# Weights and columns of a float32r matmul stream at other addresses, and its three passes in another order

## The chip, the cores and the metric

The kernel runs on one core of a Trainium2 chip. The metric is the device time of one execution in microseconds (us). Several executions are timed; one of them, a separate one, is profiled.

## What is computed

The reference is the trunk of a two-layer encoder. It has 272 positions (16 meta tokens ahead of 256 inputs), each of 2,048 features, in float32. Layer 0 mixes with a state-space scan, layer 1 with an attention that takes its keys and values from the output of layer 0; each is followed by a gated feed-forward stage. At the end the 16 meta positions are dropped.

```python
h = concatenate([meta, x])                                   # 272 x 2048
h = h + ssd_mixer(rmsnorm(h))                                # in_proj 2048 -> 10304, scan, out_proj 4096 -> 2048
h = h + (silu(u @ w_gate) * (u @ w_up)) @ w_down             # 2048 -> 2 x 5632 -> 2048
k, v = rmsnorm(h) @ w_kv                                     # 2048 -> 2 x 2048
h = h + stick_breaking_attention(rmsnorm(h) @ w_q, k, v) @ w_o
h = h + swiglu(rmsnorm(h))                                   # the second feed-forward stage
return rmsnorm(h)[16:]
```

Nearly all of the arithmetic is in the products with weight matrices.

## The kernel before, in words

The kernel keeps features on the 128 partitions and positions along the free dimension. A weight matrix is cut into 128x128 tiles. One output tile (128 features by all positions) is the sum over the K tiles of the contraction: K is 16 for an input of 2,048 features, 44 for the hidden layer of a feed-forward stage, 8 for a piece of the out projection.

**Three passes.** A float32 product is made of three float32r products. Every weight tile w is split into wh (rounded) and wl (the rest), every input x into xh and xl, and `mac` (L108 to L112) adds wh·xh (L110), wh·xl (L111) and wl·xh (L112) into one accumulator. Each `PE.matmul` is two instructions of TensorE: a load of 128x128 weights (LDWEIGHTS, engine PEld in the profile) and a matmul (PE) that streams the columns of x through them. While a matmul streams, the load of the next one's weights runs. So the load beside the pass on L110 is that of wh once more, the load beside L111 is that of wl, and the load beside L112 is that of the next tile's wh.

**Where the weights come from.** `load` (L91) brings eight weight tiles, 512 KB, into one of five `raw` buffers through the SP queue. `halves` (L99) makes `hi` with a copy on ScalarE (L101) into one of five buffers, and `lo` with a subtraction on VectorE (L103) into one of four. `project` (L114) makes one output tile, `project_block` (L130) several together. All engines run through their own instructions in order; a scheduler in the build decides that order, and waits on semaphores tie the engines together.

**The inputs.** They are held split, as one tile of shape [128, K, 2, n]: for each k first the n columns of xh, then the n columns of xl. `split_scaled` (L150) writes them for u, the input of each stage. Other inputs are y (output of the scan), hid (hidden layer), ukv (input of keys and values), uq (of the queries) and ob (output of the attention). n is 272 (T) in layer 0 and for keys and values, and 256 (SEQ) for queries, attention and the second feed-forward stage.

**Addresses in a partition.** A weight tile has 512 bytes, and `hi` and `lo` buffers start at 81,920 and 102,400 plus multiples of 4,096. So every load of weights starts at a multiple of 256 bytes. u and ukv start at 26,624 (0 beyond a multiple of 256), hid and uq at 126,400 (192 beyond), ob at 159,168 (192), the two y tiles at 132,672 and 150,080 (64). With 256 columns a half takes 1,024 bytes, so all columns of a stage start equally far beyond a multiple of 256. With 272 columns a half takes 1,088 bytes, which is 64 beyond a multiple of 256, so the start moves by 64 bytes from one half to the next.

**Distance.** In this text the distance of a load is the address of the weights loaded minus the address of the columns that the matmul in flight reads, taken modulo 256. In the program before it is:

| input | columns | distance of the loads beside L110, L111, L112 |
|---|---|---|
| u (second feed-forward stage) | 256 | 0, 0, 0 |
| hid (second feed-forward stage), uq, ob | 256 | 64, 64, 64 |
| u (layer 0), ukv | 272 | k even: 0, 192, 0; k odd: 128, 64, 128 |
| hid (first feed-forward stage), y | 272 | 64, 0, 64 and 192, 128, 192 by turns |

**The scan beside the projections.** In layer 0 the scan of one group of heads (`ssd_scan`, L339) is a generator whose steps are put between the projections of the next group (`pump`). It loads `et`, `elast` and `ef` from a buffer in DRAM through the SP queue (L361, L380), takes their exponent on ScalarE (L404 to L406) and reads `ef` last on VectorE (L431). `ef` has two buffers here, and so have `ga` (L414) and `rg` (L435).

## Time and profile before

| | |
|---|---|
| median of 3 runs | 2716.47 us (2715.73 to 2719.71) |
| the profiled execution | 2715.76 us |
| its span, first to last instruction | 2714.0 us |
| mean granted TensorE clock | 0.998 |
| PE busy, PEld busy | 2700.6 us, 2685.5 us |
| VectorE (DVE), ScalarE (ACT) busy | 1605.6 us, 1307.1 us |
| matmul instructions | 22,112 |
| read from HBM | 475.67 MB, 176 GB/s over the span |

How to read it: matmuls are pipelined, and one of them is shown as busy for about 0.28 us although the next starts 0.12 us later. So what a matmul costs isn't its duration. It is the time from its start to the start of the next one: the length of a stretch in which PE does nothing else, divided by the matmuls in it. The count that the profile gives for a stretch includes about 2 matmuls that started before it. Lines such as L110 are lines of the kernel before; in the kernel after the change the three passes stand on L127, L128 and L129, the copies that make `hi` on L114.

### The profile page before, as it was taken

The page shows a single profiled execution, that of the slowest core. Times are in us where ns is not written, and L with a number is a line of the kernel's source. Part 1 is how long each engine was busy: PE and PEld are TensorE (multiplying, and loading weights), DVE is VectorE, ACT ScalarE, POOL GpSimd, SP SyncE. Part 2 cuts the span into 40 slices and gives each one's busy share as a digit, 9 for nine tenths or more (in the row PEclk, how much of TensorE's full clock was granted, in tenths as well). Part 3 has the DMA queues.
Part 4 walks back from the last instruction along what each step waited for, and adds up shares of the span by engine and source line. Part 5 has one row for each costly group of instructions (what it writes and reads, how often), then busy time and mean ns, then how long its engine had stood idle before and what let it go on. Part 6 is the DMA issues. An engine that isn't in the chain of part 4 may idle for free.

```text
span 2714.0 us, 52235 instructions
## 1 busy us (share of the span) xinstructions
PE 2700.6 (100%) x22112; PEld 2685.5 (99%) x22112; DVE 1605.6 (59%) x2220; ACT 1307.1 (48%) x1792; POOL 5.5 (0%) x22
## 2 busy tenths in 40 slices
PE   9999999999999999999999999999999999999998
PEld 9999999999999999999999999999999999999998
DVE  8777767668755555555444655555655555554554
ACT  7766566645544444444343544444544444443443
POOL 0000000000000000000000000000000000000000
PEclk9999999999999999999999999999999999999999
DMA  6755555654555555555555555555665666565664
GB/s 224 225 177 177 177 171 177 180 170 155 173 177 174 176 172 177 174 176 175 172 175 174 173 172 158 156 156 162 193 181 184 182 186 181 185 182 177 204 195 138
DMA packets 156235, 481.24 MB, mean 177 GB/s; under 512 B 18720, under 2 KB 39776, under 8 KB 156000
## 3 DMA queue, kind: packets, MB, share of 16 engines
q1 hardware_dynamic: 155712, 477.62, 57.3%
q8 instruction: 173, 2.83, 0.4%
q14 instruction: 62, 0.51, 0.1%
q10 hardware_dynamic: 288, 0.28, 0.0%
HBM read 475.67 MB, written 2.17 MB: 176 GB/s over the span
## 4 chain that ended last, share of the span: by engine, by line
PE 99%; DVE 0%; DMA 0%; ACT 0%; issue 0%; DVEq 0%; SPq 0%; ACTq 0%
PE pp L110 31%; PE pp L112 31%; PE pp L111 31%; PE py L422 1%; PE py L424 1%; PE pt L349 0%; PE po L571 0%; PE po L570 0%; PE psc L545 0%; PE pr L170 0%; DMA et<-cumD 0%; DMA raw<-w_first 0%; PE pe L110 0%; PE pe L112 0%; PE pe L111 0%; DVE o L642 0%
## 5 line engine op out<-in xcount | busy, mean ns | idle before, releaser
L101 ACT CAST hi<-raw 128x1024 fp32r<-128x1024 f32 (+1 forms) x899 | 928.5, 1034 | 1231.2 <-PE pp L111 994.9
L103 DVE TENSOR_TENSOR lo<-raw,hi 128x1024 fp32r<-128x1024 f32 (+1 forms) x899 | 1076.4, 1199 | 502.3 <-PE pp L112 280.9
L110 PE MATMUL pp<-u,hi 128*128 128x272 f32 (+1 forms) x4064 | 1166.7, 287 | 0.5 <-ACT hi L101 0.5
L112 PE MATMUL pp<-u,lo 128*128 128x272 f32 (+1 forms) x4064 | 1165.3, 287 | 0.2 <-DVE lo L103 0.2
L111 PE MATMUL pp<-u,hi 128*128 128x272 f32 (+1 forms) x4064 | 1163.2, 286 | 0.0
L111 PEld LDWEIGHTS pp<-u,hi 128*128 128x128 f32 x4064 | 775.3, 191 | 0.2
L110 PEld LDWEIGHTS pp<-u,hi 128*128 128x128 f32 x4064 | 769.4, 189 | 1.2 <-ACT hi L101 0.7
L112 PEld LDWEIGHTS pp<-u,lo 128*128 128x128 f32 x4064 | 768.9, 189 | 1.2 <-DVE lo L103 0.8
L110 PE MATMUL pp<-hid,hi 128*128 128x272 f32 (+1 forms) x1408 | 397.0, 282 | 0.0
L112 PE MATMUL pp<-hid,lo 128*128 128x272 f32 (+1 forms) x1408 | 396.4, 282 | 0.0
L111 PE MATMUL pp<-hid,hi 128*128 128x272 f32 (+1 forms) x1408 | 396.1, 281 | 0.0
L111 PEld LDWEIGHTS pp<-hid,hi 128*128 128x128 f32 x1408 | 265.3, 188 | 0.0
L110 PEld LDWEIGHTS pp<-hid,hi 128*128 128x128 f32 x1408 | 264.6, 188 | 0.0
L112 PEld LDWEIGHTS pp<-hid,lo 128*128 128x128 f32 x1408 | 264.3, 188 | 0.0
L110 PE MATMUL pp<-ukv,hi 128*128 128x272 f32 x512 | 149.0, 291 | 0.0
L110 PE MATMUL pp<-y,hi 128*128 128x272 f32 x512 | 148.7, 290 | 0.0
L112 PE MATMUL pp<-ukv,lo 128*128 128x272 f32 x512 | 147.6, 288 | 0.0
L111 PE MATMUL pp<-y,hi 128*128 128x272 f32 x512 | 147.4, 288 | 0.0
L111 PE MATMUL pp<-ukv,hi 128*128 128x272 f32 x512 | 147.4, 288 | 0.0
L112 PE MATMUL pp<-y,lo 128*128 128x272 f32 x512 | 147.1, 287 | 0.0
L145 DVE TENSOR_TENSOR gt<-pp,rB 128x272 f32<-128x272 f32 (+1 forms) x88 | 38.1, 433 | 145.0 <-PE pp L112 145.0
L145 DVE TENSOR_TENSOR ut<-pp,rB 128x272 f32<-128x272 f32 (+1 forms) x88 | 38.1, 433 | 144.0 <-PE pp L112 144.0
(218 smaller groups left out, 2602.2 us busy)
## 6 DMA issues: line engine op xcount, KB each, us to landing
raw<-w_gu SPq DMA_DIRECT2D x352, 512.0 KB, 3.6
raw<-w_down SPq DMA_DIRECT2D x160, 512.0 KB, 3.8
raw<-w_in SPq DMA_DIRECT2D x152, 512.0 KB, 3.6
raw<-w_out SPq DMA_DIRECT2D x64, 512.0 KB, 3.7
raw<-w_kv SPq DMA_DIRECT2D x64, 512.0 KB, 3.6
raw<-w_q SPq DMA_DIRECT2D x32, 512.0 KB, 3.6
raw<-w_o SPq DMA_DIRECT2D x32, 512.0 KB, 3.6
raw<-w_down SPq DMA_DIRECT2D x32, 256.0 KB, 2.6
```

The lines of the kernel that those rows point to most:

```text
L101: S.copy(hi[:, :n, :m], raw[:, :n, :m])
L103: V.tensor_tensor(out=lo[:, :n, :m], in0=raw[:, :n, :m], in1=hi[:, :n, :m].bitcast(F32), op=ALU.subtract)
L110: PE.matmul(ps[:, :n], wh, xh, start=first, stop=False)
L111: PE.matmul(ps[:, :n], wh, xl, start=False, stop=False)
L112: PE.matmul(ps[:, :n], wl, xh, start=False, stop=last)
L145: V.tensor_tensor(out=dst, in0=ps[:, :r.shape[-1]], in1=r, op=ALU.mult)
L422: PE.matmul(py[i * HD:(i + 1) * HD, c0:c1], xd[b][:, 2 * j + i, :], gm[b][:, 2 * j + i, :], start=b < 2, stop=b != 1)
L424: PE.matmul(py[:, T:T + T - OQ], xw[:, 2 * j:2 * j + 2, :], cb[:, OQ:T], start=True, stop=True)
```

## The change

The change does these things.

1. `mac` runs the passes in the order wh·xl, wh·xh, wl·xh. The loads beside them are those of wh, wl and the next wh, as before.
2. An input is no longer [128, K, 2, n]. `pair` makes one tile that holds all K pieces of xl and behind them all K pieces of xh, with a pad ahead and a gap between.
3. `hi` and `lo` buffers are 8 x 144 floats wide in place of 8 x 128. With 272 columns a weight tile starts every 576 bytes (64 beyond a multiple of 256); with 256 columns every 512 bytes, and then `lo` starts 192 bytes into its buffer.
4. A small tile `gap` and the pads put the starts in place. The built program has, for example, u at 25,600, `hi` at 80,960 plus multiples of 4,608 and `lo` at 104,064 plus multiples of 4,608. By these addresses every load of weights but about 100 (in the first pieces of u) has the distance 64, in every stage.
5. To make room, `ef`, `ga` and `rg` have one buffer in place of two, and `diag` moves to another pool.

```diff
+PAD = {"u": 0, "u2": 0, "y": 48, "uq": 16, "ob": 0, "hid": (16, 16)}
...
+        for tag, bufs in (("raw", RAW), ("hi", 5)):
+            wp.tile([P, 8 * P if tag == "raw" else WC * 144], F32 if tag == "raw" else F32R, tag=tag, name=f"{tag}_", bufs=bufs)
+        wp.tile([P, 16], F32, name="gap")
...
         def halves(raw, n, m=P):
-            hi = wp.tile([P, WC, P], F32R, tag="hi", name=nm("hi"), bufs=5)
+            st = STEP[0]
+            hi = wp.tile([P, WC * 144], F32R, tag="hi", name=nm("hi"), bufs=5)
+            hi = hi[:, :WC * st].rearrange("p (k c) -> p k c", c=st)
+            lo = wp.tile([P, WC * 144], F32R, tag="lo", name=nm("lo"), bufs=4)
+            o = 0 if st > P else 48
+            lo = lo[:, o:o + WC * st].rearrange("p (k c) -> p k c", c=st)
             S.copy(hi[:, :n, :m], raw[:, :n, :m])
-            lo = wp.tile([P, WC, P], F32R, tag="lo", name=nm("lo"), bufs=4)
...
+        def pair(pool, K, n, pad, gap, **kw):
+            t = pool.tile([P, pad + 2 * K * n + gap], F32R, **kw)
+            return [t[:, o:o + K * n].rearrange("p (k t) -> p k t", t=n) for o in (pad + K * n + gap, pad)]
+
         def mac(ps, hi, lo, j, x, k, first, last, m=P):
-            n = x.shape[-1]
-            wh, wl, xh, xl = hi[:, j, :m], lo[:, j, :m], x[:, k, 0, :], x[:, k, 1, :]
-            PE.matmul(ps[:, :n], wh, xh, start=first, stop=False)
-            PE.matmul(ps[:, :n], wh, xl, start=False, stop=False)
+            n = x[0].shape[-1]
+            wh, wl, xh, xl = hi[:, j, :m], lo[:, j, :m], x[0][:, k, :], x[1][:, k, :]
+            PE.matmul(ps[:, :n], wh, xl, start=first, stop=False)
+            PE.matmul(ps[:, :n], wh, xh, start=False, stop=False)
             PE.matmul(ps[:, :n], wl, xh, start=False, stop=last)
 
         def project(src, x, m=P, o=None, then=None):
-            K = x.shape[1]
+            K = x[0].shape[1]
...
+            STEP[0] = 144 if x[0].shape[-1] == T else P
...
-        u = upool.tile([P, KD, 2, T], F32R, tag="u", name="u0")
+        u = pair(upool, KD, T, PAD["u"], 16, tag="u", name="u0")
...
-            ybuf = [q0.tile([P, 2 * GT, 2, T], F32R, name=f"y{i}") for i in range(2)]
+            ybuf = [pair(q0, 2 * GT, T, PAD["y"], 16, name=f"y{i}") for i in range(2)]
...
-                ef = q2.tile([P, GT, T - OQ], F32, tag="ef", name=nm("ef"))
+                ef = q2.tile([P, GT, T - OQ], F32, tag="ef", name=nm("ef"), bufs=1)
...
-                ga = sp.tile([P, T], F32, tag="ga", name=nm("ga"))
+                ga = sp.tile([P, T], F32, tag="ga", name=nm("ga"), bufs=1)
...
-                rg = sp.tile([P, T], F32, tag="rg", name=nm("rg"))
+                rg = sp.tile([P, T], F32, tag="rg", name=nm("rg"), bufs=1)
...
-                hid = fp.tile([P, KF, 2, n], F32R, name=f"hid{layer}")
+                hid = pair(fp, KF, n, PAD["hid"][layer], 16 * (1 - layer), name=f"hid{layer}")
...
-            uq = b1p.tile([P, KD, 2, SEQ], F32R, name="uq")
+            uq = pair(b1p, KD, SEQ, PAD["uq"], 0, name="uq")
...
-            ob = b1p.tile([P, KD, 2, SEQ], F32R, name="ob")
+            ob = pair(b1p, KD, SEQ, PAD["ob"], 0, name="ob")
...
-            u = upool.tile([P, KD, 2, SEQ], F32R, tag="u", name="u2")
+            u = pair(upool, KD, SEQ, PAD["u2"], 0, tag="u", name="u2")
...
-        diag = cp.tile([P, 2, P], F32, name="diag")
+        diag = sp.tile([P, 2, P], F32, name="diag", bufs=1)
```

The one buffer of `ef` changes which load stands at a place of the SP queue. Between the second and the third group's projections it holds, before (the name at the left of the arrow is the buffer written, `raw` are weights):

```order
L361 DMA et_1917<-cumD 128x8x144
L96 DMA raw_1957<-w_in 128x1024
L361 DMA et_2727<-cumD 128x8x128
L361 DMA elast_730<-cumD 16x8x16
L96 DMA raw_1987<-w_in 128x1024
L380 DMA ef_2732<-cumD 64x4x144 x2
L96 DMA raw_2034<-w_in 128x1024
```

And after the change, at the same place:

```order
L380 DMA et_1920<-cumD 128x8x144
L98 DMA raw_1960<-w_in 128x1024
L380 DMA et_2730<-cumD 128x8x128
L380 DMA elast_733<-cumD 16x8x16
L98 DMA raw_1990<-w_in 128x1024
L399 DMA ef_1923<-cumD 64x4x144 x2
L98 DMA raw_2037<-w_in 128x1024
```

The load of `ef` stands at the same place among the weights, but before it is that of the third group (`ef_2732` belongs with `et_2727`), and now it is that of the second (`ef_1923` with `et_1920`); the second group's came earlier in the program before.

ScalarE takes the exponent of that `ef`. Before, behind the same load, its rows have none:

```order
L101 CAST hi_1880<-raw_1878 128x1024
L368 ACTIVATE et_1917<-et_1917,cumT 128x144
L368 ACTIVATE et_2727<-et_2727,cumT 128x128
L404 ACT_TABLE_LOAD
L404 ACTIVATE et_1917<-et_1917 128x1152
L303 ACTIVATE ca_1758<-xin_465,cw 128x272
L443 CAST y_473<-zs_737 128x272 x4
L101 CAST hi_1959<-raw_1957 128x1024
```

After the change the exponent stands between two of the copies that make `hi`:

```order
L114 CAST hi_1883<-raw_1881 128x8x128
L387 ACTIVATE et_1920<-et_1920,cumT 128x144
L425 ACT_TABLE_LOAD
L425 ACTIVATE ef_1923<-ef_1923 128x576
L462 CAST y_476<-zs_740 128x272
L114 CAST hi_1962<-raw_1960 128x8x128
L322 ACTIVATE ca_1761<-xin_468,cw 128x272
```

So ScalarE's next copy of weights, `hi_1962` (before `hi_1959`), now stands behind an exponent that needs the late `ef`. In the stages with 272 columns the copies and subtractions write eight rows of 128 (128x8x128) in place of one run of 1,024; with 256 columns they write one run as before. On TensorE the order of tiles stays, but for a few transposes that trade places at the end of the scan, and names and shapes are the same; that a row on L127 now reads xl and one on L128 xh is seen in the diff alone.

More of the change, by code (lines that the diff above doesn't have):

```diff
@@ L84, in trunk @@
         uid = [0]
+        STEP = [144]
         def nm(s):
@@ L130, in project_block @@
         def project_block(srcs, x, then=None):
-            K = x.shape[1]
+            K = x[0].shape[1]
             pss = [pp.tile([P, 512], F32, tag="pp", name=nm("pp")) for _ in srcs]
+            STEP[0] = 144 if x[0].shape[-1] == T else P
             for k0 in range(0, K, WC):
@@ L150, in split_scaled @@
         def split_scaled(dst, k, src, gcol):
-            S.activation(dst[:, k, 0, :], src, AF.Identity, scale=gcol)
-            V.scalar_tensor_tensor(out=dst[:, k, 1, :], in0=src, scalar=gcol,
-                                   in1=dst[:, k, 0, :].bitcast(F32),
+            S.activation(dst[0][:, k, :], src, AF.Identity, scale=gcol)
+            V.scalar_tensor_tensor(out=dst[1][:, k, :], in0=src, scalar=gcol,
+                                   in1=dst[0][:, k, :].bitcast(F32),
                                    op0=ALU.mult, op1=ALU.subtract)
@@ L442, in ssd_scan @@
                                            op0=ALU.mult, op1=ALU.mult)
-                    S.copy(yb[:, j, 0, :], zs[:, j, :])
-                    V.tensor_tensor(out=yb[:, j, 1, :], in0=zs[:, j, :], in1=yb[:, j, 0, :].bitcast(F32),
+                    S.copy(yh[:, j, :], zs[:, j, :])
+                    V.tensor_tensor(out=yl[:, j, :], in0=zs[:, j, :], in1=yh[:, j, :].bitcast(F32),
                                     op=ALU.subtract)
@@ L467, in trunk @@
             pump(100)
-            u = upool.tile([P, KD, 2, T], F32R, tag="u", name="u1")
+            u = pair(upool, KD, T, PAD["u"], 16, tag="u", name="u1")
             out_project(6, u)
@@ L487, in ffn @@
                     V.tensor_tensor(out=ut, in0=ut, in1=gt, op=ALU.mult)
-                    S.copy(hid[:, m, 0, :], ut)
-                    V.tensor_tensor(out=hid[:, m, 1, :], in0=ut, in1=hid[:, m, 0, :].bitcast(F32),
+                    S.copy(hid[0][:, m, :], ut)
+                    V.tensor_tensor(out=hid[1][:, m, :], in0=ut, in1=hid[0][:, m, :].bitcast(F32),
                                     op=ALU.subtract)
@@ L499, in finish0 @@
             if m == 0:
-                ukv[0] = upool.tile([P, KD, 2, T], F32R, tag="u", name="ukv")
+                ukv[0] = pair(upool, KD, T, PAD["u"], 16, tag="u", name="ukv")
             residual(h[:, m, :], ps)
@@ L572, in attend @@
                 PE.matmul(po[:, 128:SEQ], vb[:, 1, :], ab[:, 256:384], start=False, stop=True)
-                S.copy(ob[:, m, 0, :], po[:, :SEQ])
-                V.tensor_tensor(out=ob[:, m, 1, :], in0=po[:, :SEQ], in1=ob[:, m, 0, :].bitcast(F32),
+                S.copy(ob[0][:, m, :], po[:, :SEQ])
+                V.tensor_tensor(out=ob[1][:, m, :], in0=po[:, :SEQ], in1=ob[0][:, m, :].bitcast(F32),
                                 op=ALU.subtract)
```

2 lines of the change are left out of this document (1 added, 1 removed).

## The prediction

> **What bounds the kernel now.** I read the page first: busy times and the chain that ended last.
>
> ```profile
> span 2714.0 us, 52235 instructions
> ...
> PE 2700.6 (100%) x22112; PEld 2685.5 (99%) x22112; DVE 1605.6 (59%) x2220; ACT 1307.1 (48%) x1792; POOL 5.5 (0%) x22
> ...
> PE 99%; DVE 0%; DMA 0%; ACT 0%; issue 0%; DVEq 0%; SPq 0%; ACTq 0%
> PE pp L110 31%; PE pp L112 31%; PE pp L111 31%; PE py L422 1%; PE py L424 1%; PE pt L349 0%; PE po L571 0%; PE po L570 0%; PE psc L545 0%; PE pr L170 0%; DMA et<-cumD 0%; DMA raw<-w_first 0%; PE pe L110 0%; PE pe L112 0%; PE pe L111 0%; DVE o L642 0%
> ```
>
> TensorE is the path for 99% of the span, and the three passes are 93% of it. So the time is the number of matmuls times the time from one start to the next. Busy shares hide that spacing; busy time by stretches shows it, in stretches where PE does little but passes:
>
> ```profile
> core 0: us, PE busy (x) PEld busy (x) DVE busy (x) ACT busy (x) POOL busy (x), PEclk, DMA share, GB/s
> 37.00:60.00 23.00, 23.00 (x186) 23.00 (x185) 22.61 (x45) 16.68 (x24) 0.00 (x0) 1.00 0.40 120
> 749.00:1279.00 530.00, 530.00 (x4222) 529.92 (x4221) 283.01 (x353) 220.24 (x267) 0.00 (x0) 1.00 0.57 175
> 1280.00:1543.00 263.00, 263.00 (x2109) 263.00 (x2108) 125.85 (x143) 105.21 (x127) 0.00 (x0) 1.00 0.57 176
> 1901.00:1952.00 51.00, 51.00 (x452) 51.00 (x452) 33.65 (x49) 26.89 (x39) 0.00 (x0) 1.00 0.63 195
> 1955.00:2462.00 507.00, 507.00 (x4226) 506.95 (x4225) 279.88 (x353) 220.23 (x268) 0.00 (x0) 1.00 0.60 183
> 2463.00:2701.00 238.00, 238.00 (x2103) 238.00 (x2102) 115.35 (x124) 103.05 (x125) 0.00 (x0) 1.00 0.59 179
> ```
>
> Two matmuls of each count began before the stretch. The rows are, in order: u in the scan layer, u and hid of the first feed-forward stage (272 columns); ob, u and hid of the second (256 columns).
>
> - 272 columns: 23/184 = 125.0 ns, 530/4220 = 125.6 ns, 263/2107 = 124.8 ns.
> - 256 columns: ob 51/450 = 113.3 ns, u 507/4224 = 120.0 ns, hid 238/2101 = 113.3 ns.
>
> The last three are the find. Same instructions, same columns, clock 1.00 in all, DMA share about 0.6 in all, yet u takes 6.7 ns more per matmul. It isn't the length of the contraction: ob has K = 16 like u, and hid 44. What tells them apart is the distance of the loads (table above): 0 for u, 64 for ob and hid. The timeline of u shows that load and columns are read together; the load begins 0.01 us behind the matmul's start:
>
> ```profile
> 2300.04 0.28 PE L111 MATMUL pp<-u,hi 128*128 128x256 f32 x1
> 2300.05 0.19 PEld L112 LDWEIGHTS pp<-u,lo 128*128 128x128 f32 x1
> 2300.16 0.28 PE L112 MATMUL pp<-u,lo 128*128 128x256 f32 x1
> 2300.17 0.19 PEld L110 LDWEIGHTS pp<-u,hi 128*128 128x128 f32 x1
> ```
>
> With 272 columns the distances change from pass to pass, and the spacing changes with a period of six:
>
> ```profile
> 899.86 0.29 PE L110 MATMUL pp<-u,hi 128*128 128x272 f32 x1
> 899.99 0.29 PE L111 MATMUL pp<-u,hi 128*128 128x272 f32 x1
> 900.12 0.29 PE L112 MATMUL pp<-u,lo 128*128 128x272 f32 x1
> 900.25 0.28 PE L110 MATMUL pp<-u,hi 128*128 128x272 f32 x1
> 900.37 0.29 PE L111 MATMUL pp<-u,hi 128*128 128x272 f32 x1
> 900.49 0.29 PE L112 MATMUL pp<-u,lo 128*128 128x272 f32 x1
> 900.62 0.29 PE L110 MATMUL pp<-u,hi 128*128 128x272 f32 x1
> ```
>
> Three matmuls (distances 0, 192, 0) take 0.39 us, the next three (128, 64, 128) 0.37. So the address matters here too, beyond the columns' own time.
>
> **The change part by part.** *256 columns.* hid, ob and uq had distance 64 and keep it: 0. u goes from 0 to 64, from 120.0 to 113.3 ns. The groups give the counts, for one of three passes each:
>
> ```profile
> L110 PE MATMUL pp<-u,hi 128*128 128x272 f32 x2656 | 768.1, 289 | 0.5 <-ACT hi L101 0.5
> ...
> L110 PE MATMUL pp<-u,hi 128*128 128x256 f32 x1408 | 398.6, 283 | 0.0
> ...
> L110 PE MATMUL pp<-hid,hi 128*128 128x272 f32 x704 | 202.6, 288 | 0.0
> ...
> L110 PE MATMUL pp<-ukv,hi 128*128 128x272 f32 x512 | 149.0, 291 | 0.0
> L110 PE MATMUL pp<-y,hi 128*128 128x272 f32 x512 | 148.7, 290 | 0.0
> ```
>
> 3 x 1408 = 4,224 matmuls by 6.7 ns (120.03 less 113.28, 6.75 unrounded) give 28.5 us.
>
> *272 columns.* No stretch of before has the distance 64 throughout, so the new spacing is bounded: not under 113.3 ns (sixteen columns more at no cost), and, if it goes in proportion to the columns, 113.3 x 272/256 = 120.4. I take 120.0, close to the upper end: part of the 113.3 belongs to the instruction and doesn't grow, but columns seem to set the pace. Of 4,384 products (2656 + 704 + 512 + 512) I leave out 64, those of the first pieces, which wait for their weights. hid: 2,112 matmuls x (124.8 - 120.0) = 10.1 us. The rest: 3 x (4384 - 64 - 704) = 10,848 x 5.6 = 60.7 us, with u's 125.6 for ukv and y too. At 120.4 it would be 5.2 us less.
>
> *Clock.* The granted clock is 1.00 at 113.3 ns per 256 columns, as dense as the new stages would be (120.0 per 272), so I cost nothing for the throttle.
>
> *The single buffer of ef.* It adds a wait: the second group's load on SP now needs the first group's last read, on VectorE. The SP row ahead of which the raw loads queue up stood there before too (it was the third group's load, and waited for the same read). New is ScalarE's exponent, with the copies of hi queued behind it.
>
> ```profile
> 128.98 0.30 DVE L431 TENSOR_TENSOR yt<-yt,ef 128x144 f32<-128x144 f32 x1
> ...
> 129.31 1.24 SPq L380 DMA_DIRECT2D ef<-cumD  x2
> ...
> DMA to landing us min/median/max: 4.1/4.7/7.5
> ...
> 135.89 1.28 ACT L404 ACT_TABLE_LOAD   x1
> ...
> 140.03 1.05 ACT L101 CAST hi<-raw 128x1024 fp32r<-128x1024 f32 x1
> ...
> 151.41 0.37 PE L110 MATMUL pp<-u,hi 128*128 128x272 f32 x1
> ```
>
> Read 128.98, second half issued by 130.55, landed 7.5 us later at worst: 138.1. The exponent's place is behind the table load at 135.89, which ends at 137.18; so ScalarE waits 0.9 us at most, and the copy whose product PE starts at 151.41 ends at 141.08, 10.3 us ahead. That lead hides it: cost 0 (uncovered, seven groups x 0.9 = 6 us). ga and rg get their next writer a whole group later: 0.
>
> *Strided copies.* The work per buffer on ScalarE and VectorE:
>
> ```profile
> L103 DVE TENSOR_TENSOR lo<-raw,hi 128x1024 fp32r<-128x1024 f32 x863 | 1051.6, 1220 | 444.8 <-PE pp L112 227.2 <-issue 202.5 <-ACT hi L101 6.3
> L101 ACT CAST hi<-raw 128x1024 fp32r<-128x1024 f32 x863 | 906.4, 1052 | 1190.6 <-PE pp L111 969.3 <-issue 211.6 <-PE pp L112 3.7
> ```
>
> Writing eight runs isn't shown anywhere in before; between a few per cent less and, say, a fifth more, 1.2 and 1.05 us stay under the 24 x 120 ns = 2.9 us that PE spends on a buffer. They lie beside PE: cost 0. The stretch 37 to 60 us, with VectorE busy 22.61 of 23.00, has no room, and there a slower subtraction would show: 0 to 2 us. The order of passes makes each stage's first matmul wait for VectorE's half where it waited for ScalarE's; five stages, 0 to 1 us each, taken as 0.
>
> *Sum.* 28.5 + 10.1 + 60.7 = 99.3 us off the profiled 2715.76 (its span 2714.0 and 1.8 around it): 2616.5. The median of the runs shown is 0.7 above the profiled execution, and some 150 matmuls into other accumulators that I left out are worth about as much the other way. Forecast 2616 us.
>
> **The Trainium skill.** Against u's 120.0 and hid's 113.3 ns stands a rule of "TensorE: Matmul & The Clock Gate" (Part 2, step 1): the array reads weights and streamed columns through two independent ports, and loading the next weights takes nothing from the running matmul. By that rule the change gives nothing and the sum is 2716 us. The trace differs, since spacing follows the distance; the rule is rival 4 below. The same page (Part 1) puts the spacing of warm matmuls at the columns over 2.4 GHz plus 2.5 ns: estimated by it, 109.2 ns for 256 and 115.8 for 272. Here 113.3 is the best that the rows show for 256; with the page's 115.8 the sum would come to about 2562 us.
>
> **The rivals.** (1) *Distance to the load's own columns.* If the load is also disturbed by the start of the matmul that uses it, one pass in three (wh with xh, 0 apart in the new layout for 272 columns) pays u's 6.7 ns: 12,960/3 x 6.75 = 29.2 us less gain, 2645. Against it: with 256 columns the two distances are the same, so before can't show it. (2) *The load of weights sets the pace*, not the columns: then 272 columns also take 113.3 ns, and 10,848 x 12.3 + 2,112 x 11.5 + 28.5 = 186 us go, 2530. Against it: spacing with 272 columns never comes near it. (3) *With 272 columns nothing is gained*, because the columns' start still moves by 64 bytes from tile to tile: only u's 28.5 us, 2687. For it: hid's loads beside L110 and L112 have 64 half the time, and its mean is still 124.8. (4) *Placement does nothing*, u's stage is slow for another reason: 2716. Against it: three inputs at 113.3 and one at 120.0 with nothing else to tell them apart. (5) *Slower.* The dear half of the period of six, 0.39 us for three, is where columns start at multiples of 256; if in the new layout every start fell into such a state with 272 columns, they would take 130 ns: 10,848 x 4.4 + 2,112 x 5.2 = 58.7 lost, less 28.5: 2746. It decides from 28.5/12,960 = 2.2 ns above today's, about 127.7 ns.
>
> **How the numbers follow.** Forecast 0.71; (1) 0.10; (2) 0.07; (3) 0.06; (4) 0.02; (5) 0.04. The forecast's own range is 2600 to 2630 us: 118.9 to 121 ns with 272 columns, and up to some 9 us of waits. With (1) it reaches to 2650, and 0.81 lies inside 2600 to 2650. About 0.2% is what a measurement of this kernel tells from no change. Faster: 0.71 + 0.10 + 0.07 + 0.06 = 0.94. Same: 0.02. Slower: 0.04.
>
> **What would show it.** In the profile after: u of the second feed-forward stage at 113 ns per matmul (about 479 us for 4,224), hid and ob of 256 columns unchanged, u and hid of the first feed-forward stage at 120 ns, with no period of six. PE idle stays at a few us. If u of the second stage stays at 120, the distance isn't the cause; if only the stages with 272 columns miss their 120.0, it's the bound above that fails; if PE waits for hi or lo in the scan layer, it's the covers.

## The result and the profile after

| | before | after |
|---|---|---|
| median of 20 runs | 2716.11 us (2715.16 to 2719.71) | 2696.31 us (2695.38 to 2727.9) |
| ratio, 95% interval | | 0.993 (0.9917 to 0.9943) |
| span of the profiled execution | 2714.0 us | 2693.8 us |

The change gained 19.8 us where 100 were forecast. One of the 20 runs took 2727.9 us, some 31 us more than the others; e4 below comes back to it.

The page of the kernel after shows the same picture as before: the busy times, the shares of the chain that ended last, and the two groups that make `hi` and `lo`.

```profile
span 2693.8 us, 52240 instructions
PE 2680.7 (100%) x22112; PEld 2666.0 (99%) x22112; DVE 1602.8 (59%) x2220; ACT 1306.9 (49%) x1792; POOL 5.5 (0%) x22
PE 99%; DVE 0%; ACT 0%; DMA 0%; issue 0%; DVEq 0%; SPq 0%
L114 ACT CAST hi<-raw 128x1024 fp32r<-128x1024 f32 (+1 forms) x899 | 928.2, 1034 | 1211.1 <-PE pp L128 982.2
L115 DVE TENSOR_TENSOR lo<-raw,hi 128x1024 fp32r<-128x1024 f32 (+1 forms) x899 | 1076.8, 1199 | 494.2 <-PE pp L129 284.0
```

PE is the path for 99% of the span again, with 22,112 matmuls again. So the 20 us are a matter of spacing alone. Busy time by stretches of the kernel after, in order: u and hid of the first feed-forward stage (272 columns); ob, u and hid of the second (256 columns). The columns are the stretch, its length, and for each engine busy time and count.

```profile
751.00:1283.00 532.00, 532.00 (x4219) 531.92 (x4218) 282.66 (x352) 219.20 (x267) 0.00 (x0) 1.00 0.56 174
1284.00:1549.00 265.00, 265.00 (x2104) 265.00 (x2103) 125.23 (x143) 104.38 (x127) 0.00 (x0) 1.00 0.56 173
1911.00:1962.00 51.00, 51.00 (x452) 51.00 (x451) 32.86 (x46) 26.49 (x37) 0.00 (x0) 1.00 0.63 196
1963.00:2441.00 478.00, 478.00 (x4218) 477.95 (x4218) 276.62 (x353) 220.59 (x268) 0.00 (x0) 1.00 0.63 194
2442.00:2681.00 239.00, 239.00 (x2111) 239.00 (x2110) 115.80 (x125) 103.55 (x125) 0.00 (x0) 1.00 0.58 179
```

With two matmuls less in each count, as in the prediction:

| input | before | after | forecast |
|---|---|---|---|
| u, second feed-forward stage (256) | 120.0 ns | 478/4216 = 113.4 | 113.3 |
| hid, second feed-forward stage; ob (256) | 113.3; 113.3 | 239/2109 = 113.3; 51/450 = 113.3 | unchanged |
| u, first feed-forward stage (272) | 125.6 | 532/4217 = 126.2 | 120.0 |
| hid, first feed-forward stage (272) | 124.8 | 265/2102 = 126.1 | 120.0 |

In sum: 4,224 x 6.65 = 28.1 us gained with 256 columns. Lost with 272 columns: 10,848 x 0.56 + 2,112 x 1.25 = 8.7 us, if ukv and y went as u did. That is 19.4 of the 20.2 us between the two spans. The gain came where it was forecast and to the size forecast; the 70.8 us that were to come from 272 columns did not come at all.

The timeline of u with 272 columns shows that the period of six is gone; it is one of twelve now (the start of the columns moves by 64 bytes from one k to the next, so it comes back after four k of three passes each):

```profile
899.74 0.29 PE L127 MATMUL pp<-u,hi 128*128 128x272 f32 x1
899.87 0.29 PE L128 MATMUL pp<-u,hi 128*128 128x272 f32 x1
900.00 0.29 PE L129 MATMUL pp<-u,lo 128*128 128x272 f32 x1
...
901.25 0.29 PE L127 MATMUL pp<-u,hi 128*128 128x272 f32 x1
```

Twelve matmuls take 1.51 us, 126 ns each. The rows are rounded to 10 ns; the starts themselves, over all of this u, give 125.2 ns from L127 to the next start, 128.7 from L128 and 124.4 from L129, and the same within 0.1 in hid. So the pass on L128, wh·xh, is the dearest by 3.9 ns over the mean of the other two. Within one pass the step also goes with the place of the columns, though the distance of the load is 64 each time: L127 takes 124, 127, 128 and 123 ns where its columns start 0, 64, 128 and 192 bytes beyond a multiple of 256.

### The profile page after: what moved, and what is told of

It reads as the page before. It is cut to its first block, busy times and chain, and to the rows that moved or that the text cites. A ratio compares the mean times of both kernels' runs of the same rounds, so it can differ in the third digit from the quotient of the medians.

```text
span 2693.8 us, 52240 instructions
## 1 busy us (share of the span) xinstructions
PE 2680.7 (100%) x22112; PEld 2666.0 (99%) x22112; DVE 1602.8 (59%) x2220; ACT 1306.9 (49%) x1792; POOL 5.5 (0%) x22
## 4 chain that ended last, share of the span: by engine, by line
PE 99%; DVE 0%; ACT 0%; DMA 0%; issue 0%; DVEq 0%; SPq 0%
PE pp L128 32%; PE pp L127 31%; PE pp L129 31%; PE py L441 1%; PE py L443 1%; PE pt L368 0%; PE po L589 0%; PE po L590 0%; PE psc L564 0%; PE pr L189 0%; PE pe L128 0%; PE pe L127 0%; PE pe L129 0%; DVE o L661 0%; PE psc L563 0%; PE pc L401 0%
## 5 line engine op out<-in xcount | busy, mean ns | idle before, releaser
L114 ACT CAST hi<-raw 128x1024 fp32r<-128x1024 f32 (+1 forms) x899 | 928.2, 1034 | 1211.1 <-PE pp L128 982.2
L115 DVE TENSOR_TENSOR lo<-raw,hi 128x1024 fp32r<-128x1024 f32 (+1 forms) x899 | 1076.8, 1199 | 494.2 <-PE pp L129 284.0
L128 PE MATMUL pp<-u,hi 128*128 128x272 f32 (+1 forms) x4064 | 1159.0, 285 | 0.0
L127 PE MATMUL pp<-u,hi 128*128 128x272 f32 (+1 forms) x4064 | 1157.7, 285 | 0.2 <-ACT hi L114 0.2
L129 PE MATMUL pp<-u,lo 128*128 128x272 f32 (+1 forms) x4064 | 1151.3, 284 | 0.0
L129 PEld LDWEIGHTS pp<-u,lo 128*128 128x128 f32 x4064 | 763.9, 188 | 0.6 <-DVE lo L115 0.2
L128 PEld LDWEIGHTS pp<-u,hi 128*128 128x128 f32 x4064 | 764.1, 188 | 0.2
L127 PEld LDWEIGHTS pp<-u,hi 128*128 128x128 f32 x4064 | 762.9, 188 | 0.9 <-ACT hi L114 0.4
L128 PE MATMUL pp<-hid,hi 128*128 128x272 f32 (+1 forms) x1408 | 398.6, 283 | 0.0
L127 PE MATMUL pp<-hid,hi 128*128 128x272 f32 (+1 forms) x1408 | 397.6, 282 | 0.0
L129 PE MATMUL pp<-hid,lo 128*128 128x272 f32 (+1 forms) x1408 | 396.4, 282 | 0.0
L129 PEld LDWEIGHTS pp<-hid,lo 128*128 128x128 f32 x1408 | 264.7, 188 | 0.0
L128 PEld LDWEIGHTS pp<-hid,hi 128*128 128x128 f32 x1408 | 264.6, 188 | 0.0
L127 PEld LDWEIGHTS pp<-hid,hi 128*128 128x128 f32 x1408 | 264.2, 188 | 0.0
L127 PE MATMUL pp<-ukv,hi 128*128 128x272 f32 x512 | 149.2, 292 | 0.0
L128 PE MATMUL pp<-y,hi 128*128 128x272 f32 x512 | 148.8, 291 | 0.0
L127 PE MATMUL pp<-y,hi 128*128 128x272 f32 x512 | 148.6, 290 | 0.0
L128 PE MATMUL pp<-ukv,hi 128*128 128x272 f32 x512 | 148.5, 290 | 0.0
L129 PE MATMUL pp<-ukv,lo 128*128 128x272 f32 x512 | 146.9, 287 | 0.0
L129 PE MATMUL pp<-y,lo 128*128 128x272 f32 x512 | 146.9, 287 | 0.0
```

What stands on the lines that cost most here:

```text
L114: S.copy(hi[:, :n, :m], raw[:, :n, :m])
L115: V.tensor_tensor(out=lo[:, :n, :m], in0=raw[:, :n, :m], in1=hi[:, :n, :m].bitcast(F32), op=ALU.subtract)
L127: PE.matmul(ps[:, :n], wh, xl, start=first, stop=False)
L128: PE.matmul(ps[:, :n], wh, xh, start=False, stop=False)
L129: PE.matmul(ps[:, :n], wl, xh, start=False, stop=last)
```

## The experiments

**The theory and its rival after the result.** Theory: the distance of the load sets the spacing, but how spacing depends on it differs between 272 and 256 columns. Rival: the distance is only one condition, and something that the table of distances doesn't hold decides too (the order of events, or the moving start of the columns).

**e1_scan.** The tiles of gate and up read weights and columns at planned places, so that each output tile has one number of columns, one distance, and a start that stands still (advance 0) or moves from matmul to matmul. Weights and columns are then not those of the stage, so its values aren't the reference's.

```diff
+                for j in range(c):
+                    for p in range(3):
+                        i = 3 * (k0 + j) + p
+                        w0 = min(j, WC - 2) * P + adv * i % 256 // 4
+                        x0 = 4416 + 256 * ((k0 + j) % 14) + (64 + adv * (i + 1) - dist) % 256 // 4
...
-                    times(gt, pre.pop(0) if pre else project(gu[m], u), r)
+                    times(gt, pre.pop(0) if pre else scan_project(gu[m], u, n, xf, plan[m - 2]), r)
```

> The kernel after the change, but 84 output tiles of each feed-forward stage (gate and up, from the third pair on) read columns and weights at addresses set by a plan, so that their values are not the reference's: each pair of output tiles has a number of columns, a distance of the load, and an advance (bytes by which columns and weights move on from matmul to matmul, modulo 256). Each place of the plan has 96 matmuls, read as the mean time from start to start. Theory 'moving start': the distance rule holds for 272 columns too, but only while the columns start at the same place modulo 256 each time: 120 ns at 272 columns, distance 64, advance 0, and 126.7 at distance 0; 256 columns with an advance of 64 bytes then lose their 113.3 and cost 118 or more. Theory 'count': the 17th block of 64 bytes itself is what costs; 272 columns take 125 to 126 ns at every distance and advance, and 256 columns with an advance of 64 still take 113.3 at distance 64. Theory 'seam': what counts is that one matmul's columns begin where those before ended; 272 columns with an advance of 64 take 120, with an advance of 0 about 126. All three: 256 columns, advance 0, take 120.0 at distance 0 and 113.3 at 64; what lies between is not known.

Means from the starts of each piece's matmuls, in ns (a piece is a pair of output tiles, 96 matmuls):

| distance, start fixed | 0 | 16 | 32 | 48 | 64 | 80 | 96 | 128 | 160 | 192 | 224 | 240 |
|---|---|---|---|---|---|---|---|---|---|---|---|---|
| 256 columns | 119.7 | 117.3 | 118.3 | 119.1 | 117.8 | 119.2 | 118.7 | 119.3 | 119.9 | 117.8 | 116.7 | 115.0 |
| 272 columns | 125.3 | 123.3 | 126.7 | 126.7 | 123.3 | 123.3 | 123.5 | 126.6 | 126.7 | 126.7 | 125.7 | 124.5 |

Busy time by stretches in this kernel, for 288 columns at distances 64 to 160 and for 320 columns at nearly all distances:

```profile
2028.00:2090.00 62.00, 62.00 (x467) 62.00 (x466) 31.09 (x39) 23.99 (x30) 0.00 (x0) 1.00 0.52 164
2130.00:2280.00 150.00, 150.00 (x1025) 150.00 (x1024) 67.90 (x86) 52.74 (x65) 0.00 (x0) 1.00 0.48 149
```

62/465 = 133.3 ns and 150/1023 = 146.6: 13.3 ns for 32 columns, 0.417 ns for one. The dearest pieces of four sizes lie on that line: 120.0 ns with 256 columns, 126.7 with 272, 133.3 with 288, 146.7 with 320; other pieces lie below it (304 columns: 137.7 and 138.7). By this slope, an estimate, the columns alone are worth 106.7 ns with 256 and 113.3 with 272, and the rest is an extra per matmul: 6.6 ns at 113.3 and 13.3 at 120.0 (256 columns). The dearest extra is 13.3 in all four sizes. With 272 columns in this kernel, at distances 0, 64 and 128 with the start fixed, and at 0 with the start moving by 192 bytes from matmul to matmul:

```profile
912.00:922.00 10.00, 10.00 (x82) 10.00 (x81) 5.83 (x7) 4.34 (x6) 0.00 (x0) 1.00 0.63 189
960.00:970.00 10.00, 10.00 (x83) 10.00 (x83) 6.03 (x8) 4.52 (x6) 0.00 (x0) 1.00 0.55 186
996.00:1006.00 10.00, 10.00 (x81) 10.00 (x80) 5.60 (x7) 4.08 (x6) 0.00 (x0) 1.00 0.54 174
1174.00:1184.00 10.00, 10.00 (x85) 10.00 (x84) 5.95 (x7) 4.44 (x6) 0.00 (x0) 1.00 0.55 181
```

A count of about 80 is uncertain by one, 1.5 ns; the starts themselves give 125.3, 123.3, 126.6 and 121.7. The last is the least that any piece with 272 columns took, an extra of 8.4 ns, and its distance is 0, the dear one with 256. Distance 64 with a fixed start has an extra of 10.0; where the start moved by 64 bytes from one matmul to the next the piece took 126.0, and in the kernel after, where it moves from one k to the next, 126.1: an extra of 12.8. Two things follow. No tried placement of 272 columns reaches the 120.0 of the forecast. And with 256 columns distance 64 gave 117.8 here, while ob, hid and the new u have 113.3 at that very distance: distance alone doesn't decide. (One piece of the table mixes two levels: at 240 its two tiles took 116.7 and 113.5.)

**e2_u2_only.** The kernel before with one edit: u of the second feed-forward stage starts 192 bytes later, at distance 64.

```diff
-            u = upool.tile([P, KD, 2, SEQ], F32R, tag="u", name="u2")
+            u = upool.tile([P, 48 + KD * 2 * SEQ], F32R, tag="u", name="u2")
+            u = u[:, 48:].rearrange("p (k h t) -> p k h t", k=KD, h=2)
```

> The kernel before, with one edit: u of the second feed-forward stage (256 columns) starts 192 bytes later, so that its loads have the distance 64. Nothing else is changed. If the gain of the change comes from this stage alone and the stages with 272 columns lose a little: the 4,224 matmuls go from 120.0 to 113.3 ns, 28.2 us less, 2688 us, about 8 us faster than the full change. If the gain needs the order of passes or the other layout: the stage stays at 120.0 and the time at 2716 us.

Measured: 2718.85 us (11 runs), ratio 1.0002 (0.9993 to 1.0011). Nothing of the 28 us. Its stretches of ob, u and hid (256 columns):

```profile
1912.00:1963.00 51.00, 51.00 (x436) 51.00 (x435) 31.62 (x45) 25.38 (x36) 0.00 (x0) 1.00 0.61 187
...
1975.00:2455.00 480.00, 480.00 (x4077) 480.00 (x4077) 269.94 (x344) 210.14 (x258) 0.00 (x0) 1.00 0.61 187
2456.00:2704.00 248.00, 248.00 (x2108) 248.00 (x2108) 115.95 (x125) 103.36 (x125) 0.00 (x0) 1.00 0.56 172
```

51/434 = 117.5, 480/4075 = 117.8, 248/2106 = 117.8 ns. u gained 2.2 ns only; and hid, whose addresses are those of before, where it took 113.3, lost 4.5. 4,224 x 2.2 = 9.3 us gained, and 2,112 x 4.5 = 9.5 lost in hid and 695 x 4.4 = 3.1 in ob (its first 73 matmuls, ahead of a wait, were as before): the gain is gone. So distance 64 with 256 columns has two levels, 113.3 and 117.8, at identical addresses.

**e3_all_but_u2.** The other half: the kernel after with u of the second feed-forward stage back at distance 0.

```diff
-PAD = {"u": 0, "u2": 0, "y": 48, "uq": 16, "ob": 0, "hid": (16, 16)}
+PAD = {"u": 0, "u2": 16, "y": 48, "uq": 16, "ob": 0, "hid": (16, 16)}
```

> The kernel after the change, with one edit: u of the second feed-forward stage has a pad of 64 bytes, so that its loads have the distance 0 again. If the gain comes from this stage alone, all of it goes and a loss is left: the stage back at 120.0 ns, 28.2 us more than the full change, 2724 us, which is 8 us slower than the kernel before. If the order of passes or the layout of xl and xh gave the gain, the stage stays at 113.3 ns and the time at 2696 us.

Measured: 2724.64 us (10 runs), ratio 1.0025 (1.0015 to 1.0034). Its stretches of u and hid:

```profile
1967.00:2473.00 506.00, 506.00 (x4217) 505.94 (x4216) 279.81 (x353) 220.08 (x268) 0.00 (x0) 1.00 0.60 183
2474.00:2713.00 239.00, 239.00 (x2111) 239.00 (x2110) 115.86 (x125) 103.67 (x125) 0.00 (x0) 1.00 0.58 179
```

506/4215 = 120.0 and 239/2109 = 113.3. u starts at a multiple of 256 in the kernel before (120.0) and in the kernel after (113.4), and 64 bytes beyond one here (120.0): it is the place relative to the weights that counts, not the columns' own. Without the new place of u the change is a loss: 8.5 us from the 2716.11 of the result, where 8.7 were worked out above, and 6.2 from the kernel before as it ran beside e3 (2718.45). So all of the gain is u's, and the changed kernel's other edits cost.

**e4_after_again.** The unedited kernel after, for more of its runs.

> The kernel after the change, unedited, beside the next three. Theory 'address': the distance alone sets the spacing; u and hid of the second feed-forward stage take 113.3 ns in every execution, 2696 us. Theory 'two states': at distance 64 the stream of matmuls has two states that hold themselves, 113.3 and 117.8 ns, and a pause of TensorE (one of about 1 us lies in the stage of ob) draws which of them follows; then some executions lie about 4.4 ns x 6,336 = 28 us higher, at 2724 to 2728 us.

Measured: 2696.17 us (12 runs, two of them at 2727.4), ratio 0.9947 (0.9923 to 0.9971). With the 20 above, 3 of 32 runs lie near 2727. If u, hid and ob of 256 columns went to 117.8 in them, they would take (4,224 + 2,112 + 768) x 4.4 = 31.3 us more: 2727.5. No profile fell on such a run, so this stays an argument. But e3's profile shows the beginning of it. Up to u of the second stage e3 has the instructions and addresses of the kernel after, and yet its ob took 51/433 = 117.8 ns where the kernel after has 113.3:

```profile
1912.00:1963.00 51.00, 51.00 (x435) 51.00 (x434) 31.75 (x46) 25.36 (x37) 0.00 (x0) 1.00 0.61 186
```

The first 73 matmuls of ob are alike in both; then PE waits 0.7 us for the attention, and behind that wait the levels part. In the same way e2, e8 and e11 have the program of the kernel before up to there, which went on at 113.3, and went on at 117.8. So equal instructions at equal addresses took either level in different runs. In e3 and in the kernel before u follows at distance 0, and hid is back at 113.3; ob's 695 matmuls cost 3.1 us, and e3's runs do lie near 2724.5 (eight) or 2727.6 (two, the profiled one among them). In the kernel after no stage at distance 0 follows.

**e5_pauses.** The kernel after; ahead of each up tile of both feed-forward stages a small matmul reads the gate's result, so that PE stands idle for some 1.4 us. All addresses stay.

```diff
+            if after is not None:
+                PE.matmul(o[:, :P], ones, after[:, :P], start=True, stop=True)
...
-                    times(ut, pre.pop(0) if pre else project(gu[KF + m], u), r)
+                    times(ut, pre.pop(0) if pre else project(gu[KF + m], u, after=gt), r)
```

> The kernel after the change, with one edit: in both feed-forward stages the first matmul of each up tile waits for the gate tile's activation (a small matmul reads it ahead of the tile, into the same accumulator, which is then overwritten), so that TensorE pauses for about 1 us 44 times in each stage. Addresses and everything else stay. Theory 'address': between the pauses u of the second stage (256 columns) takes 113.3 ns in all 44 pieces, and u of the first stage (272 columns) 126.1 in all. Theory 'two states': the 44 pieces of 256 columns fall into two groups, 113.3 and 117.8 ns, at the same addresses; for 272 columns there may be more than one state too, with 126.1 among them.

One run, 2878.04 us. A pause as the timeline shows it, and four stretches between pauses: two with 272 columns, two with 256.

```profile
2082.22 0.28 PE L129 MATMUL pp<-u,lo 128*128 128x256 f32 x1
2083.88 0.49 PE L136 MATMUL pp<-gt,ones 128*128 128x128 f32 x2 [1.38 <-ACT gt L505]
```

```profile
783.50:795.00 11.50, 11.50 (x94) 11.50 (x93) 4.82 (x6) 3.57 (x4) 0.00 (x0) 1.00 0.49 141
797.50:809.00 11.50, 11.50 (x94) 11.50 (x93) 4.82 (x6) 3.57 (x4) 0.00 (x0) 1.00 0.50 144
2071.50:2082.00 10.50, 10.50 (x95) 10.50 (x94) 4.70 (x6) 3.58 (x4) 0.00 (x0) 1.00 0.54 159
2084.50:2095.00 10.50, 10.50 (x91) 10.50 (x91) 4.77 (x6) 3.58 (x4) 0.00 (x0) 1.00 0.54 151
```

The last two have the same length and 95 and 91 matmuls: 113.3 and 117.8 ns by their starts, 13 us apart, with the same instructions at the same places modulo 256 (the weights go round five and four buffers). Of the 43 pieces with 256 columns 7 have 113.3 (the first, the second, and from there every seventh), and 36 have 117.8. All 43 pieces with 272 columns have 126.1. So with 256 columns a pause draws one of two levels anew, and within a piece it holds. With 272 columns the 126.1 is no unlucky draw: it is the one level that this layout showed.

**e6_after_starter and e7_u2_starter.** Before each run of distance 64 in u and w_o, the first pieces are put at distance 0 by weights that lie 192 bytes later; e6 in the kernel after, e7 on top of e2. The thought behind it: distance 0 leads into the level of 113.3, since hid had it behind u at distance 0 in the kernel before.

```diff
-            hi = hi[:, :WC * st].rearrange("p (k c) -> p k c", c=st)
+            hi = hi[:, sh:sh + WC * st].rearrange("p (k c) -> p k c", c=st)
...
-                    hi, lo = halves(load(src, k0, c), c)
+                    hi, lo = halves(load(src, k0, c), c, sh=48 if (K, x[0].shape[-1]) == (KD, SEQ) else 0)
```

> The kernel after the change, with one edit: the first four output tiles of the attention's out projection and of the second feed-forward stage have their weights 192 bytes later, at the distance 0; all others stay at 64. Theory 'two states' with the addition that a stretch at distance 0 always leads into the fast state (as it did between u and hid of the second stage in the kernel before): u and hid of the second stage take 113.3 ns in every execution, 2696 plus 384 x 6.7 ns = 2.6 us, about 2697 to 2699 us, with no execution near 2727. If distance 0 doesn't choose the state, the spread is that of the unedited kernel beside it. Theory 'address': 2699 us, and the unedited kernel beside it always at 2696.

> The kernel before with u of the second feed-forward stage 192 bytes later (as in the run with that edit alone, which stayed at 2718.9 us), and with the first four tiles of the out projection and of this stage at the distance 0, as in the run above. If distance 0 leads into the fast state: u takes 113.3 ns in place of 117.8, hid too, and the stages with 272 columns keep the spacing of before (125.5); 2716 - 27 us = about 2688 to 2690 us, faster than both kernels. If it doesn't: 2716 to 2720 us, as without it.

Measured: 2727.8 us (5 runs), ratio 1.0045 (1.0033 to 1.0057), and 2719.67 us (11 runs), ratio 1.0015 (1.0006 to 1.0024). The stretch of u in e6:

```profile
1990.00:2465.00 475.00, 475.00 (x4035) 475.00 (x4034) 265.66 (x336) 206.51 (x252) 0.00 (x0) 1.00 0.61 187
```

475/4033 = 117.8 ns: here distance 0 led to the worse level, and in e7 too. The thought falls as it was put. e6 does two other things: it turns the changed kernel's whole gain into a loss by an edit of its first pieces, and it lands where the stray runs of e4 lie, 2727.

**e10_states.** What goes ahead, by itself: as e1, with 24 matmuls ahead of each pair of gate and up tiles whose distance is another, by columns that lie later or by weights that lie later (its values aren't the reference's either). What the table calls a level is a state in the expectation.

```diff
+                if k0 == 0 and pre is not None:
+                    scr = prp.tile([P, 512], F32, tag="pr", name=nm("lead"))
+                    for j in range(24):
+                        w0 = j % 7 * P + pre[1] // 4
+                        x0 = 4416 + 256 * (j % 13) + (64 - dist) % 256 // 4 + pre[0] // 4
+                        PE.matmul(scr[:, :n], hi[:, w0:w0 + P], xf[:, x0:x0 + n], start=True, stop=True)
```

> The kernel after the change with the gate and up tiles of both feed-forward stages at planned addresses as in the first scan (values are not the reference's), fixed starts throughout; ahead of each pair 24 matmuls run whose columns or weights start some bytes further on, so that each pair begins out of another distance. First stage 272 columns, second stage 256. Theory 'the way into the distance fixes the state': at 256 columns and distance 64 the pairs fall into 113.3 and 117.8 ns by what goes ahead, the same each time that the same goes ahead. For 272 columns the question is whether any way leads to 120.0, the value forecast: if none of 14 at distance 64 and none at 0, 32, 128 and 192 does, the forecast's step from 256 to 272 columns has no state to stand on, and spacing stays at 123 to 127 ns. Theory 'count': 272 columns, one value whatever goes ahead.

One run, 2922.86 us. Five stretches at distance 64 with 256 columns: nothing ahead (behind a pair at 117.8), columns 64 bytes later ahead, twice, and weights 192 bytes later ahead, twice.

```profile
2327.00:2337.00 10.00, 10.00 (x87) 10.00 (x86) 5.72 (x7) 4.25 (x6) 0.00 (x0) 1.00 0.54 185
2341.00:2351.00 10.00, 10.00 (x91) 10.00 (x90) 4.01 (x4) 3.48 (x4) 0.00 (x0) 1.00 0.42 140
2355.00:2364.50 9.50, 9.50 (x86) 9.50 (x86) 4.01 (x4) 3.48 (x4) 0.00 (x0) 1.00 0.41 138
2382.50:2392.50 10.00, 10.00 (x87) 10.00 (x86) 4.01 (x4) 3.46 (x4) 0.00 (x0) 1.00 0.38 134
2411.00:2421.00 10.00, 10.00 (x88) 10.00 (x86) 4.01 (x4) 3.47 (x4) 0.00 (x0) 1.00 0.39 127
```

87, 91, 86 in 9.5 us, 87, 88 matmuls: slow, fast, fast, slow, slow. By their starts:

| | ahead | level |
|---|---|---|
| 256 columns, distance 64 | columns +64 (distance 0) | 113.3 in 8 of 8 |
| | weights +192 (distance 0) | 117.8 in 4 of 4 |
| | nothing | that of the pair ahead is kept |
| 256 columns, distance 0 | anything | 120.0 in 7 of 7 |
| 272 columns, distance 64 | anything | 123.3 to 123.4 in 14 of 14 |
| 272 columns, distances 128, 192 | anything | 126.6 to 126.7 in 14 of 14 |
| 272 columns, distances 0, 32 | various | 125.3 to 125.5 in 9 of 14, 126.6 to 126.7 in 5 |

Columns +64 and weights +192 are the same distance, 0, and lead to different levels. Distances 96 and 128 did the same, with one piece each way: out of the same level, moved columns led to 117.8 and moved weights to 113.3. This fits e6 and e7, whose starter moved the weights. With 256 columns distance 0 has one level and distance 64 two that keep themselves; distance 192 showed both as well. With 272 columns distance 64 has one, and distances 0 and 32 showed two, 125.4 and 126.7.

**e8_u2_lead and e9_after_lead.** The lead that gave 113.3 in 8 of 8 (24 matmuls at distance 0 by columns 64 bytes later), put ahead of the fifth output tile of w_o; e8 on top of e2, e9 in the kernel after.

```diff
+                if k0 == 0 and lead is not None:
+                    scr = prp.tile([P, 512], F32, tag="pr", name=nm("lead"))
+                    for j in range(24):
+                        PE.matmul(scr[:, :SEQ], hi[:, j % 8, :P], lead[:, 16 + SEQ * (j % 8):16 + SEQ * (j % 8 + 1)],
+                                  start=True, stop=True)
...
-                finish_o(m, project(a["w_o"][m], ob))
+                finish_o(m, project(a["w_o"][m], ob, lead=obf if m == FILLERS else None))
```

> The kernel before with u of the second feed-forward stage 192 bytes later (distance 64), and with 24 matmuls at distance 0 put ahead of the out projection's fifth output tile; they read columns 64 bytes further on, into an accumulator that nothing reads. So the switch from 0 to 64 is made by the columns' start moving back by 64 bytes, as between u and hid of the second stage in the kernel before, and not by the weights' start as in the two runs with a starter (which went to 117.8 ns each time). Theory 'the way into distance 64 fixes the state': ob's later tiles, u and hid of the second stage take 113.3 ns in every execution, about 2716 - 28 + 3 = 2688 to 2692 us, faster than both kernels. Theory 'only a pause sets the state': the 24 matmuls change nothing, 117.8 ns and 2719 to 2723 us.

> The kernel after the change with the same 24 matmuls at distance 0 ahead of the out projection's fifth output tile. Theory 'the way into distance 64 fixes the state': 113.3 ns in all later 256-column stages, 2696 to 2699 us in every execution, without the ones near 2727 that the unedited kernel has (3 of 32). Theory 'only a pause sets the state': the spread of the unedited kernel, some executions near 2727 to 2730.

e8: 2718.51 us (11 runs), ratio 1.0007 (0.9999 to 1.0016). Its stretches: ob behind the lead, the beginning of u, the rest of u.

```profile
1935.00:1957.00 22.00, 22.00 (x197) 22.00 (x196) 14.19 (x21) 11.31 (x16) 0.00 (x0) 1.00 0.65 197
1959.00:1969.00 10.00, 10.00 (x91) 10.00 (x90) 5.35 (x6) 4.25 (x6) 0.00 (x0) 1.00 0.63 192
...
1980.00:2455.00 475.00, 475.00 (x4036) 475.00 (x4035) 265.65 (x336) 206.90 (x252) 0.00 (x0) 1.00 0.61 187
```

22/195 = 112.8, 10/89 = 112.4 (by the starts 113.3 in both; short counts are uncertain by one) and then 475/4034 = 117.8. The lead worked, through ob and the first 96 matmuls of u; there the norm's own small matmul (it makes 1/rms) comes between, and from it on the level is 117.8 until the end. So the level changed at an event on TensorE, in the middle of one input. In the kernel after the same small matmul stands at the same place and leaves 113.3 as it is; why, is open. e9: 2698.84 us (5 runs, 2698.38 to 2699.3), ratio 0.9934 (0.9921 to 0.9948), 113.3 in all later stages. 24 more matmuls account for the 2.7 us over the kernel after (e4). None of its five runs was near 2727, which at 3 in 32 says little.

**e11_u2_lead2 and e12_fixed_starts.** e11 is e2 with the lead behind that small matmul, ahead of the third gate tile. e12 is e11, and halves of u and ukv with 272 columns lie 1,280 bytes apart in place of 1,088, so that their starts no longer move and the distance is 64 (`RAW` is 4 and `ef`, `ga`, `rg` have one buffer, for room).

```diff
-                    times(gt, pre.pop(0) if pre else project(gu[m], u), r)
+                    times(gt, pre.pop(0) if pre else project(gu[m], u, lead=uflat[0] if uflat and m == 2 else None), r)
```

```diff
-RAW = 5
+RAW = 4
...
-        u = upool.tile([P, KD, 2, T], F32R, tag="u", name="u0")
+        u = upool.tile([P, 64 + KD * 2 * 320], F32R, tag="u", name="u0")
+        u = u[:, 48:48 + KD * 2 * 320].rearrange("p (k h t) -> p k h t", k=KD, h=2)[:, :, :, :T]
```

> The kernel before with u of the second feed-forward stage 192 bytes later (distance 64), and 24 matmuls at distance 0 ahead of that stage's third gate tile, which is behind the norm's small matmul that moved the run before last from 113.3 to 117.8 ns. Theory 'two states, the way in decides': from there on u and hid take 113.3 ns; 4,032 x 6.7 = 27.0 us less in u, the first 192 at up to 117.8, 2.9 us more for the 24: 2716 - 25 = about 2690 to 2693 us in every execution, faster than both kernels; hid stays at its 113.3. If the state can't be set this way: 2718 to 2722 us.

> The run above, and in addition u and ukv of the stages with 272 columns keep 1,280 bytes for each half, so that all their columns start equally far beyond a multiple of 256, at distance 64 (with four raw buffers in place of five, and one of ef, ga and rg, for the room). Nothing else moves. Theory 'fixed starts': u of the scan layer, u of the first feed-forward stage and ukv go from 125.5 to the 123.3 ns that the scans showed for this geometry, 9,456 x 2.2 = 21 us less, about 2670 us. The forecast's 120.0 would need 52 us less, about 2640. If 272 columns cost the same at any addresses: 2691 us as in the run above.

e11: 2694.58 us (4 runs, 2690.74 to 2694.98), ratio 0.9913 (0.99 to 0.9927). Its u and hid of 256 columns:

```profile
1990.00:2440.00 450.00, 450.00 (x3973) 450.00 (x3972) 258.68 (x330) 204.60 (x249) 0.00 (x0) 1.00 0.63 194
2441.00:2680.00 239.00, 239.00 (x2111) 239.00 (x2110) 115.83 (x125) 103.58 (x125) 0.00 (x0) 1.00 0.57 179
```

450/3971 = 113.3 and 239/2109 = 113.3. Against e8, where 24 such matmuls stand ahead of the norm, this is 24 us, with all stages at the same distances: the order of events makes it. e12: 2674.53 us (5 runs, 2671.24 to 2675.07), ratio 0.9838 (0.9824 to 0.9851); the kernel before took 2717.37 beside it. Its u and hid of the first feed-forward stage, u and hid of the second:

```profile
742.00:1262.00 520.00, 520.00 (x4217) 519.92 (x4216) 282.50 (x352) 219.86 (x267) 0.00 (x0) 1.00 0.58 178
1263.00:1526.00 263.00, 263.00 (x2109) 263.00 (x2108) 125.93 (x143) 105.34 (x127) 0.00 (x0) 1.00 0.56 176
...
1975.00:2420.00 445.00, 445.00 (x3929) 445.00 (x3928) 256.67 (x328) 202.78 (x246) 0.00 (x0) 1.00 0.64 194
2422.00:2660.00 238.00, 238.00 (x2103) 238.00 (x2102) 115.26 (x124) 103.18 (x125) 0.00 (x0) 1.00 0.58 181
```

520/4215 = 123.4 ns where the kernel before has 125.6: 9,504 matmuls of u and ukv x 2.2 = 20.9 us, and 20.05 lie between the medians of e11 and e12. hid is unchanged (263/2107 = 124.8). e12 is the fastest of all the kernels here, 21.8 us under the 2696.31 of the kernel after, which did not run beside it.

## Why the prediction was wrong

**Right: what bounds the kernel, and u of the second feed-forward stage.** TensorE's spacing is the whole story, and u went from 120.0 to 113.4 ns, 28.1 us where 28.5 were forecast. But the reason given, "What tells them apart is the distance of the loads", was half of it. e3 shows that distance 0 costs 120.0. e2 shows that distance 64 isn't enough for 113.3. That the changed kernel gets it comes from what runs ahead, in 29 of 32 runs by their times, and so the right number for u was in part luck: the prediction had three inputs at 113.3 in one profile and took that for a property of the distance, while ob took 117.8 at the same addresses in other runs (e2, e8, e11).

**Wrong: "I take 120.0, close to the upper end".** This is the step that failed, with the bound behind it, "if it goes in proportion to the columns, 113.3 x 272/256 = 120.4". It was meant as an upper end and lay below everything that 272 columns ever showed (121.7 to 126.7). Measured, in the new layout: 126.1. Scaling 113.3 carried the small extra of 6.6 ns from 256 to 272 columns; the extra there is 12.8. 12,960 matmuls x 6.1 ns = 79 us, the miss. The rows on record held a warning, which the prediction quoted under rival (3): half of hid's loads beside two of the passes had distance 64, and hid still took 124.8. As a price it should have made 124 the end that the range reached to.

**The rivals.** (3), "With 272 columns nothing is gained", came nearest: 2687 for 2696. Its reason, the start that moves by 64 bytes, holds in part: with fixed starts distance 64 takes 123.3 to 123.4 (e10, e12), with moving ones 126.1 in every piece (e5). (In e10 and e12 wh·xh also lies 64 from its own columns, where it lies 0 from them in the kernel after; no run separates the two.) What it left out is that the moving start can be worse than before, by 0.6 ns on most matmuls and 1.3 on hid's. (1), one pass in three, has a part in it: wh·xh is the dearest pass, by 3.9 ns, and 4,320 x 3.9 = 16.8 us of the 79. It can't be the miss as a whole, since the other two passes average 124.8, not 120.0; and whether the pass is dear for its own columns isn't shown. (2), 113.3 for 272 columns: no piece came within 8 ns. (5) had the right sign for these columns and too much of it: 130 was priced, 126.7 is the most that any piece showed. (4), no effect of placement, falls with e3: one pad moved u by 6.7 ns. That was the rule of the Trainium skill, "TensorE: Matmul & The Clock Gate" (Part 2, step 1), that the two ports are independent and a load takes nothing from the running matmul; the trace disagrees, by 6.7 ns in 120. The spacing that this page of the Trainium skill gives (Part 1: the columns over 2.4 GHz plus 2.5 ns) has the columns right, 0.417 ns each as in e1, but nothing here came down to an extra of 2.5: the least were 6.6 and 8.4 ns.

**The covers held.** ScalarE's timeline in the kernel after, where the second group's `ef` is late, and PE's use of the copy behind it:

```profile
135.09 1.28 ACT L425 ACT_TABLE_LOAD   x1
136.38 0.69 ACT L425 ACTIVATE ef<-ef 128x576 f32<-128x576 f32 x1
137.28 1.04 ACT L114 CAST hi<-raw 128x1024 fp32r<-128x1024 f32 x1
...
150.79 0.37 PE L127 MATMUL pp<-u,hi 128*128 128x272 f32 x1
```

The exponent follows its table load at once, and the copy ends 12.5 us ahead of its use: cost 0, as taken. The strided copies and subtractions: 1034 and 1199 ns as the mean over all 899 buffers, and the page of before has the same 1034 and 1199 over its 899; cost 0. The clock stayed at 1.00 in all stretches.

**What stays open.** What the two levels are physically, and why the norm's small matmul switches them in e8 and not in the kernel after. Why 272 columns never have an extra of 6.6 ns, and how much of their 126.1 is the moving start and how much the own columns of wh·xh. And whether the runs near 2727 are the worse level, which the sum, e3's ob and e6 suggest and no profile of such a run shows.

## What to carry to other kernels

When equal streams show unequal spacing, change one address and leave the rest (e2 and e3, one line each) before a layout is rebuilt: it would have shown that the address is a condition and the history another. A price seen with one size isn't scaled to the next; split it first into what goes with the size and what doesn't, from two sizes at least. And where a range rests on an unmeasured bound, the nearest measured row, here hid's 124.8 with a third of its loads at the new distance, belongs inside it.

## What the runs showed of the hardware

- By the slope from 288 to 320 columns (e1) a float32r matmul with its load costs 0.417 ns for each column, and beside that an extra that depends on where weights and columns lie within 256 bytes: 6.6 to 13.3 ns with 256 columns, 8.4 to 13.4 with 272.
- At distance 64 with 256 columns there are two levels, 113.3 and 117.8 ns, that keep themselves over thousands of matmuls. They changed behind a pause (0.7 us idle in ob's stage, 1.4 in e5), at a small matmul (e8) and behind 24 matmuls of another distance (e10, e11); with pauses at near-equal intervals every seventh piece had the quick one (e5).
- The same distance, made by moving the columns or by moving the weights, leads to different levels afterwards (e10: 113.3 in 8 of 8 and 117.8 in 4 of 4): the two addresses act one by one, and not their difference alone.
